# One piece of embedding weights serves all row blocks in the last weighted stage, half of its product is kept in SBUF, and an early split comes later

## The chip, the cores and the metric

The kernel runs on one core of one Trainium2 chip. Its time is the device time of one execution in microseconds (us); three executions of the kernel before gave a median of 803.88 us, from 803.66 to 804.14. One more execution was recorded by the profiler, and all rows of a profile come from that one.

The engines are named as the profile names them: PE is TensorE (matmuls; PEld is its weight loads), DVE is VectorE, ACT is ScalarE, POOL is GpSimd, SP is SyncE, which here only starts DMAs.

## The reference

With DEPTH = 1 the reference is one attention layer, a gated embedding, and a final normalization, over 512 rows of 2048 columns, all in float32:

```python
hn = rmsnorm(x, norm_g[0])
y = swa_mixer(hn, ...)            # windowed attention, out gated, @ w_out (2048 x 2048)
x = x + y
emb = p[0] @ ple_proj[0]          # 512 x 256 @ 256 x 2048
g = jax.nn.sigmoid(rmsnorm(x, ple_norm[0]) @ ple_gate[0])   # @ 2048 x 2048
x = x + emb * g
return rmsnorm(x, final_g)
```

The change touches the last four lines: the embedding `emb`, the gate `g`, and the final gain `final_g`.

## The kernel before

**Products in three parts.** Matmuls take operands that are rounded when written as `fp32r`. So each float32 operand is split in two: `hi` is a cast on ACT, `lo = raw - hi` a subtraction on DVE. `mm3` (lines 120 to 122) then makes one float32 product of three matmuls: hi·hi, hi·lo, lo·hi. A weight piece is 128 x 1024 (512 KB): it is loaded by SP (line 568), cast (line 575) and subtracted (line 576). The raw pieces, the `hi` and the `lo` parts have three buffers each (`wpool`, `bufs=3`). So the cast of piece n has to wait until PE is done with piece n-3.

**Seven products a stage.** The two 2048 x 2048 products (`w_out`, then `ple_gate`) are made by a scheme of seven block products instead of eight. A product p works on sums of quarters of the activations (`Forms`: again a cast, line 680, and a subtraction, line 681) and on sums of weight blocks. The last stage goes through p in the order 2, 7, 1, 6, 5, 3, 4. Each p but the last is two units, `jj` = 0 and 1, of 512 columns each. One unit takes four weight pieces m = 0..3, with 12 matmuls a piece: 48 matmuls into two banks of PSUM. After each piece it lets a share of the list `later` run (`some_later`), and then calls `todo()`, which issues a step of the next forms or an early split.

**Which product ends what.** With rows in four blocks t of 128 and columns in four groups j of 512, p = 1 ends the gate of rows t = 0, 1 and columns j = jj; p = 5 that of t = 2, 3 and j = 2 + jj; p = 3 that of t = 0, 1 and j = 2 + jj; p = 4, the last, that of t = 2, 3 and j = jj. Where a gate is complete, the embedding of the same rows and columns is needed. `embed` makes one block of it: six matmuls (two chunks of 128 of the contraction, three parts each) into one bank of PSUM, with a `ple_proj` piece of 512 columns that goes through the same queue of weight pieces (`add_embeds`). So for p = 1, 5 and 3 there are five pieces to a unit, and the columns 2 + jj come through the queue twice, once for p = 5 and once for p = 3.

**What follows a unit.** `gate` and `gated` (lines 890 to 905): ACT takes the sigmoid (line 896), DVE multiplies it with the embedding (line 898) and adds that to x (line 899), ACT takes the sum of squares (line 902). These steps are put at the front of `later`, and so run between the pieces of the next unit. Two sums go through `s2` and `s7`, tiles of 128 x 2 x 2 x 512.

**The last product.** Its eight weight pieces lie in SBUF before their turn and are split early by `split_last(k)` (lines 583 and 584), at places given by the table `early`: key (p, jj, m), value k. Then four blocks of 128 rows by 512 columns follow, each of 24 matmuls (`last`) and an embedding of 6; the fourth is made in two halves. Beside them the rows that are complete are normalized: a sum over `ssq3` (line 1034 for t = 0, 1), a root on ACT, then four multiplications by the root and the gain for t = 0 (line 920), four for t = 1, and so on, and the stores by SP (line 915). The gain is `final_g`, copied to all partitions in the tile `fg` (128 x 2048, 1 MB); its load is issued in the middle of the `w_out` stage, after p = 6 (line 870).

**What sets the order.** From the second product of the last stage on, the order of all engines is the order in which the program is written (`tc.manual_schedule` with PE, SP, DVE, Activation and Pool). Each engine runs its instructions in that order, and a wait holds up all that stands behind it on the same engine.

**PSUM.** There are four tags with two banks each: `p` and `s`, `t` and `o`. For p = 5 and 3 the two gate banks of a unit are those of p = 1, in `s` and `p`; the embeddings of unit jj go to tag `"to"[jj]`.

Of the kernel before, what the change touches and what calls it, by code (L numbers as in the profile page):

```python
# [20 lines left out]
P = 128  # L21
# [32 lines left out]
def trunk_kernel(ctx: ExitStack, tc: tile.TileContext, a: dict):  # L54
    nc = tc.nc
# [25 lines left out]
    def bank(name, tag):  # L81
        return others.get(tag, psum).tile([P, 512], F32, tag=tag, name=name)


    WE = 1024
# [31 lines left out]
    def mm3(ps, sh, sl, mh, ml, first, last, more=False):  # L117


        nc.tensor.matmul(ps, sh, mh, start=first, stop=False, skip_group_check=more)  # L120
        nc.tensor.matmul(ps, sh, ml, start=False, stop=False, skip_group_check=more)  # L121
        nc.tensor.matmul(ps, sl, mh, start=False, stop=last, skip_group_check=more)  # L122
# [23 lines left out]
    def run(gen):  # L146
        for _ in gen:
            pass
# [36 lines left out]
    for k in range(KC):  # L185
# [9 lines left out]
        room = acts if k < KC // 2 else more  # L195
# [14 lines left out]
        f, e = k == 0, k == KC - 1  # L210
# [8 lines left out]
        for t in range(2):  # L219
            c = slice(t * P, (t + 1) * P)  # L220
            mm3(kt_ps[t], wh[:, c], wl[:, c], h, l, f, e)
        for t in range(NB):
            c = slice(t * P, (t + 1) * P)
# [8 lines left out]
        if 3 <= k < 3 + NB:  # L232
            t = k - 3
# [190 lines left out]
    def turn(i):  # L424


        d, g = divmod(i, UNITS)
        pr = T.pop(i)
        pt = bank(f"pt{i}", "t")[:, :256]
        for u in range(2):  # L430
            nc.tensor.transpose(pt[:, u * P : (u + 1) * P], pr[:, u, :], ident)
        r = apool.tile([P, 2, 256], F32R, tag="r", name=f"r{i}", bufs=2)
        nc.scalar.copy(r[:, 0], pt)
        nc.vector.tensor_sub(r[:, 1], pt, r[:, 0].bitcast(F32))  # L434
        own = None
        if g >= 2:
            own = apool.tile([P, 2, 256], F32R, tag="own", name=f"own{i}", bufs=2)
            rows = slice(0, P) if g % 2 else slice(0, HB)
            flat = lambda v: v[rows].rearrange("p l (u q) -> p (l u) q", q=HB)


            sign = -1 if g % 2 else 1
            nc.gpsimd.affine_select(  # L443
                out=flat(own), in_=flat(r).bitcast(F32), pattern=[[0, 8], [sign, HB]], compare_op=ALU.is_ge, fill=0.0,
                base=-HB - 1 if g % 2 else 0, channel_multiplier=-sign,
            )
            here, there = slice(HB, P), slice(0, HB)
            if g % 2 == 0:
                here, there = there, here
            nc.scalar.copy(own[there, 0], own[here, 1].bitcast(F32))  # L450
        PT[i] = (r, own)
# [76 lines left out]
    def block(nm, r, c, jj, m):  # L528
        return a[nm][2 * (c - 1) + jj, 4 * (r - 1) + m]

    SUMS = [("w_out", 7), ("w_out", 5), ("w_out", 6), ("ple_gate", 7), ("ple_gate", 5)]
    for nm, p in SUMS:
        for jj in range(2):
            for m in range(4):
                t = summed[nm, p, jj, m] = tc.dram_tile([P, WE], F32, name=f"{nm}_{p}_{jj}_{m}")
# [12 lines left out]
    class Pieces:  # L548
# [38 lines left out]
        done = 0  # L587
# [26 lines left out]
    def add_stage(nm, order):  # L614
        at = {}

        def add_embeds(p, jj):
            if nm == "ple_gate" and p in (1, 5, 3, 4):
                j = jj + 2 * (p in (5, 3))
                B.add("proj", a["ple_proj"].rearrange("(k p) d -> p k d", p=P)[:, :, j * 512 : (j + 1) * 512])  # L620

        for p in order:
            for jj in range(2):
                if nm == "ple_gate" and (p, jj) == (4, 0):
                    for v in range(2):
                        at["e", v] = len(B.specs)
                        add_embeds(p, v)
                at[p, jj] = len(B.specs)
                for m in range(4):
                    if (nm, p) in SUMS:  # L630
                        src = summed[nm, p, jj, m]
                    else:
                        src = block(nm, *{1: (1, 1), 2: (2, 1), 3: (2, 2), 6: (1, 1), 4: (2, 1)}[p], jj, m)
                    growing = (6, 4) if (nm, 6) in SUMS else (7, 6, 4)
                    kind = "seed" if p == growing[0] else "grow" if p in growing else "one"
                    B.add(kind, src, (nm, jj, m) if p in growing else None)
                if p != 4:
                    add_embeds(p, jj)
        return at
# [112 lines left out]
    fg = late.tile([P, D], F32, name="fg")  # L752
# [17 lines left out]
    later = []  # L770
# [6 lines left out]
    def unit(p, jj, at, forms, todo):  # L777

        ps = banks(p, jj, forms.nm)
        f = forms.made[p]  # L780
        first = p not in (6, 5, 3)
        for m in range(4):
            bh, bl = B.get(at[p, jj] + m)
            for kk in range(2):
                k = 2 * m + kk
                fh, fl = f[m]
                for tb in range(2):
                    mm3(ps[tb], fh[:, kk, blk(tb)], fl[:, kk, blk(tb)], bh[kk], bl[kk], first and k == 0, k == 7, not first)
            some_later(4 - m)
            todo()  # L790
        return ps


    def load_x(j):
        nc.sync.dma_start(x1[j], a["x"].rearrange("(t p) d -> p t d", p=P)[:, :, j * 512 : (j + 1) * 512])
# [48 lines left out]
    for n, p in enumerate(ORDER_OUT):  # L844
        nxt = out_forms.steps(ORDER_OUT[n + 1]) if n < 6 else iter(())
        for jj in range(2):
            later.extend(held.pop(waiting.get((p, jj)), ()))
            calls = iter(range(4))

            def todo():  # L850
                part = x_at.get((p, jj, next(calls)))
                if part is not None:
                    load_x(part)
                next(nxt, None)
                if p == 4:
                    for tag in "to":
                        if turns:
                            turn(*turns.pop(0), tag)
                    if jj:
                        next(ple_first, None)  # L860

            ps = unit(p, jj, at_out, out_forms, todo)
            posts = [partial_of(add_y, p, jj, tb, ps[tb]) for tb in range(2)]
            if p == 1:
                held[p, jj] = posts
            else:
                later.extend(posts)
        run(nxt)
        if p == 6:
            nc.sync.dma_start(fg, a["final_g"].partition_broadcast(P))  # L870
        if p == 3:
            turns = [(kp, 0) for kp in range(8)] + [(kp, 1) for kp in range(4, 8)]
    run(ple_first)
# [8 lines left out]
    nc.vector.tensor_sub(pTl, pT, pTh.bitcast(F32))  # L882
    done = {t: 0 for t in range(NB)}

    def embed(t, w, tag, c=slice(0, 512)):
        e_ps = bank(f"e{t}_{done[t]}", tag)
        for k in range(2):
            mm3(e_ps[:, c], pTh[:, k, blk(t)], pTl[:, k, blk(t)], w[0][k][:, c], w[1][k][:, c], k == 0, k == 1)
        return e_ps
# [32 lines left out]
    s2, s7 = partial("s2"), partial("s7")  # L922
    turns = [(kp, 1) for kp in range(4)]

    def gate(p, jj, ps, e):
# [17 lines left out]
                zs.append((tb, 2 + jj, ps[tb], late.tile([P, 512], F32, tag="junk", name=f"z{jj}_{tb}", bufs=3)))  # L943
        return [gated(*z, e[z[0]]) for z in zs]

    def gate_later(*v):
        zs = gate(*v)
        later[:0] = [partial_of(next, z, None) for _ in range(3) for z in zs]
# [2 lines left out]

    spare = late.tile([P, 2 * WE], F32R, name="spare")
    rooms4 = {}
    early = {(5, 0, 3): 0, (5, 1, 2): 1, (5, 1, 3): 2, (3, 0, 1): 3, (3, 0, 3): 4, (3, 1, 0): 5, (3, 1, 2): 6}

    def split_last(k):
        if k == 0:
# [7 lines left out]
    for n, p in enumerate(ORDER_PLE[:-1]):  # L965
        if n == 1:

            ctx.enter_context(
                tc.manual_schedule(
                    engines={getattr(mybir.EngineType, v) for v in ("PE", "SP", "DVE", "Activation", "Pool")}  # L970
                )
            )
        nxt = ple_forms.steps(ORDER_PLE[n + 1])
        for jj in range(2):
            calls = iter(range(4))

            def todo():
                k = early.get((p, jj, next(calls)))
                if turns:
                    turn(*turns.pop(0), "s")  # L980
                    if not turns:
                        nc.vector.tensor_reduce(ss2, ssq2, axis=AX.X, op=ALU.add)
                        run(rsqrt_mean(rstd2, ss2, D, "r2"))
                    return
                next(nxt, None)
                if p == 2:
                    next(nxt, None)
                if k is not None:
                    split_last(k)

            ps = unit(p, jj, at_ple, ple_forms, todo)
            e = {}
            if p in (1, 5, 3):
                w = B.get(at_ple[p, jj] + 4)
                for t in (0, 1) if p in (1, 3) else (2, 3):
                    e[t] = embed(t, w, "to"[jj])
            if (p, jj) != (3, 1):
                later.insert(0, partial_of(gate_later, p, jj, ps, e))
        run(nxt)
# [4 lines left out]
    w = [B.get(at_ple["e", jj]) for jj in range(2)]  # L1004
    f = ple_forms.made[4]
# [155 lines left out]
```

## Time and profile before

| what | value |
| --- | --- |
| median of three executions | 803.88 us (803.66 to 804.14) |
| the profiled execution: time, span | 804.26 us, 802.4 us |
| PE busy | 791.1 us |
| PE weight loads busy | 660.0 us |
| DVE busy | 592.1 us |
| ACT busy | 500.5 us |
| POOL busy | 110.1 us |

The span goes from the first to the last instruction; the 1.9 us between span and time lie around it. A PE that is busy all the time is one whose matmuls follow each other; a wait of PE inside a stage shows as a longer step from one start to the next. In the last stage the matmuls of 512 columns start 0.227 us apart. A busy share over the span says little on single stages, so the stage of the change has to be read by its own rows.

### The profile page before, as it was taken

How to read it: one execution, taken by the hardware profiler on the slowest of the kernel's cores; microseconds unless marked ns; L12 is line 12 of the kernel's file. 1: busy time of each engine (PE TensorE's matmuls, PEld its weight loads, DVE VectorE, ACT ScalarE, POOL GpSimd, SP SyncE). 2: the span in 40 equal slices, each digit the busy share in tenths (PEclk: the TensorE clock that was granted, in tenths of full speed). 3: DMA queues.
4: the chain of work that ended last, by engine and by line, in shares of the span. 5: the costliest groups of instructions: out<-in, count | busy, mean ns of one | idle time of the engine just before them, and what ended most of it. 6: DMA issues, size and time to landing. Idle time of an engine off the chain costs nothing. (4 is left out here: it accounts for less than half of the span.)

```text
span 802.4 us, 10946 instructions
## 1 busy us (share of the span) xinstructions
PE 791.1 (99%) x3763; PEld 660.0 (82%) x3763; DVE 592.1 (74%) x970; ACT 500.5 (62%) x1041; POOL 110.1 (14%) x218
## 2 busy tenths in 40 slices
PE   9999999999999999999999999999999999999995
PEld 7888888888888888888888888888888888888785
DVE  4536886887777776777778897766646756989896
ACT  5624667676667666676666654655668656656855
POOL 0002213122122212112122200030000020200000
PEclk9999999999999999999999999999999999999998
DMA  8863678778687977868685369898513996785532
GB/s 318 327 172 101 183 241 215 228 202 233 172 220 215 218 215 199 221 177 246 159 219 132 105 233 348 333 275 248 195 46 92 372 216 197 156 229 182 182 107 105
DMA packets 45239, 165.15 MB, mean 206 GB/s; under 512 B 5936, under 2 KB 8112, under 8 KB 41344
## 3 DMA queue, kind: packets, MB, share of 16 engines
q1 hardware_dynamic: 38352, 130.59, 47.9%
q0 software_dynamic: 6832, 33.88, 22.4%
q8 instruction: 29, 0.48, 0.2%
q14 instruction: 26, 0.21, 0.1%
HBM read 158.63 MB, written 46.19 MB: 255 GB/s over the span
## 5 line engine op out<-in xcount | busy, mean ns | idle before, releaser
L576 DVE TENSOR_TENSOR blo<-braw,bhi 128x1024 fp32r<-128x1024 f32 x80 | 97.5, 1222 | 39.7 <-ACT bhi L575 39.4
L575 ACT CAST bhi<-braw 128x1024 fp32r<-128x1024 f32 x80 | 84.0, 1051 | 65.8 <-PE g L122 18.9
L122 PE MATMUL gps<-xh,wlo 128*128 128x512 f32 x256 | 100.1, 391 | 0.0
L121 PE MATMUL gps<-xl,whi 128*128 128x512 f32 x256 | 100.1, 391 | 0.0
L120 PE MATMUL gps<-xh,whi 128*128 128x512 f32 x256 | 99.8, 390 | 0.0
L107 DVE TENSOR_TENSOR wlo<-wraw,whi 128x1024 fp32r<-128x1024 f32 x60 | 73.3, 1221 | 20.8 <-ACT whi L106 19.7
L122 PE MATMUL qps<-xh,wlo 128*128 128x512 f32 x224 | 87.8, 392 | 0.0
L120 PE MATMUL o<-bhi,fho 128*128 128x512 f32 x224 | 87.7, 391 | 0.0
L121 PE MATMUL qps<-xl,whi 128*128 128x512 f32 x224 | 87.7, 391 | 0.0
L121 PE MATMUL o<-blo,fho 128*128 128x512 f32 x224 | 87.3, 390 | 0.0
L122 PE MATMUL o<-bhi,flo 128*128 128x512 f32 x224 | 87.2, 389 | 0.0
L120 PE MATMUL qps<-xh,whi 128*128 128x512 f32 x224 | 87.2, 389 | 0.0
L106 ACT CAST whi<-wraw 128x1024 fp32r<-128x1024 f32 x60 | 62.9, 1048 | 26.9 <-PE gps L121 10.6
L418 ACT ACTIVATE t<-t,sm 128x129 f32<-128x129 f32 x128 | 50.6, 397 | 45.9 <-DVE sm L415 45.6
L121 PE MATMUL g<-blo,fhg 128*128 128x512 f32 x192 | 75.0, 391 | 0.7 <-DVE blo L576 0.7
L120 PE MATMUL g<-bhi,fhg 128*128 128x512 f32 x192 | 75.1, 391 | 0.0
L122 PE MATMUL g<-bhi,flg 128*128 128x512 f32 x192 | 74.8, 390 | 0.0
L443 POOL TENSOR_SCALAR_AFFINE_SELECT own<-r 64x512 fp32r<-64x512 f32 (+1 forms) x48 | 34.1, 711 | 291.7 <-DVE r L434 286.2
L122 PEld LDWEIGHTS gps<-xh,wlo 128*128 128x128 f32 x256 | 48.0, 188 | 10.3
L576 DVE TENSOR_TENSOR blo<-grown,bhi 128x1024 fp32r<-128x1024 f32 x32 | 39.1, 1223 | 23.6 <-ACT bhi L575 21.9
L120 PEld LDWEIGHTS gps<-xh,whi 128*128 128x128 f32 x256 | 48.1, 188 | 8.9
L121 PEld LDWEIGHTS gps<-xl,whi 128*128 128x128 f32 x256 | 48.1, 188 | 8.9
(200 smaller groups left out, 1698.0 us busy)
## 6 DMA issues: line engine op xcount, KB each, us to landing
wraw<-in_w_gate_in SPq DMA_DIRECT2D x32, 512.0 KB, 5.6
wraw<-in_w_q SPq DMA_DIRECT2D x28, 512.0 KB, 4.5
w_out<-in_w_out POOLq DMA_DIRECT2D x24, 512.0 KB, 7.4
braw<-in_w_out SPq DMA_DIRECT2D x24, 512.0 KB, 4.3
braw<-in_ple_gate SPq DMA_DIRECT2D x24, 512.0 KB, 4.3
w_out<-in_w_out SPq DMA_DIRECT2D x16, 512.0 KB, 6.7
ple_gate<-in_ple_gate SPq DMA_DIRECT2D x16, 512.0 KB, 5.5
ple_gate<-in_ple_gate POOLq DMA_DIRECT2D x16, 512.0 KB, 7.2
```

What stands on the lines that cost most here:

```text
L106: nc.scalar.copy(hi, raw)
L107: nc.vector.tensor_sub(lo, raw, hi.bitcast(F32))
L120: nc.tensor.matmul(ps, sh, mh, start=first, stop=False, skip_group_check=more)
L121: nc.tensor.matmul(ps, sh, ml, start=False, stop=False, skip_group_check=more)
L122: nc.tensor.matmul(ps, sl, mh, start=False, stop=last, skip_group_check=more)
L418: nc.scalar.activation(su, su, AF.Exp, bias=sm[:, u : u + 1], accum_out=sm[:, 2 + u : 3 + u])
L443: nc.gpsimd.affine_select(out=flat(own), in_=flat(r).bitcast(F32), pattern=[[0, 8], [sign, HB]], compare_op=ALU.is_ge, fill=0.0, base=-HB ...
L575: nc.scalar.copy(hi, raw)
L576: nc.vector.tensor_sub(lo, raw, hi.bitcast(F32))
```

## The change

The `ple_proj` pieces of p = 3 are taken out of the queue of weight pieces. While the piece of columns 2 + jj is there for p = 5, the embeddings of all four row blocks are made with it. Those of t = 2, 3 are used from PSUM as before. Those of t = 0, 1 (named `k`) go to the other tag of embedding banks, `"to"[1 - jj]`, and `keep` copies them to SBUF by ACT: for jj = 0 into the first half of `fg`, for jj = 1 into `s7[:, 0]`. The gates of p = 3 multiply with these copies. The copies are a step of `later` that is put behind the steps of the unit's own gates.

Since `fg` is a room for the copies now, the load of `final_g` is moved from the `w_out` stage to the third piece of unit (3, 1).

Four of the early splits of the last weights come later: k = 3 from (3, 0, 1) to (3, 0, 3), k = 4 from (3, 0, 3) to (3, 1, 0), k = 5 from (3, 1, 0) to (3, 1, 1), k = 6 from (3, 1, 2) to (3, 1, 3).

```diff
@@ add_embeds
-            if nm == "ple_gate" and p in (1, 5, 3, 4):
-                j = jj + 2 * (p in (5, 3))
+            if nm == "ple_gate" and p in (1, 5, 4):
+                j = jj + 2 * (p == 5)
                 B.add("proj", a["ple_proj"].rearrange("(k p) d -> p k d", p=P)[:, :, j * 512 : (j + 1) * 512])
@@ the w_out stage
         run(nxt)
-        if p == 6:
-            nc.sync.dma_start(fg, a["final_g"].partition_broadcast(P))
@@ embed
-    def embed(t, w, tag, c=slice(0, 512)):
-        e_ps = bank(f"e{t}_{done[t]}", tag)
+    def embed(t, w, tag, c=slice(0, 512), nm="e"):
+        e_ps = bank(f"{nm}{t}_{done[t]}", tag)
@@ new
+    kept = {}
+
+    def keep(jj, e):
+
+        room = s7[:, 0] if jj else fg[:, :WE].rearrange("p (t c) -> p t c", t=2)
+        kept[jj] = [room[:, t] for t in range(2)]
+        for t in range(2):
+            nc.scalar.copy(kept[jj][t], e[t])
@@ the table of early splits
-    early = {(5, 0, 3): 0, (5, 1, 2): 1, (5, 1, 3): 2, (3, 0, 1): 3, (3, 0, 3): 4, (3, 1, 0): 5, (3, 1, 2): 6}
+    early = {(5, 0, 3): 0, (5, 1, 2): 1, (5, 1, 3): 2, (3, 0, 3): 3, (3, 1, 0): 4, (3, 1, 1): 5, (3, 1, 3): 6}
@@ todo
-                k = early.get((p, jj, next(calls)))
+                at = p, jj, next(calls)
+                k = early.get(at)
+                if at == (3, 1, 2):
+                    nc.sync.dma_start(fg, a["final_g"].partition_broadcast(P))
@@ after each unit
             e = {}
-            if p in (1, 5, 3):
+            if p in (1, 5):
                 w = B.get(at_ple[p, jj] + 4)
-                for t in (0, 1) if p in (1, 3) else (2, 3):
+                for t in (0, 1) if p == 1 else (2, 3):
                     e[t] = embed(t, w, "to"[jj])
+            if p == 3:
+                e = kept[jj]
+            if p == 5:
+
+                later.insert(0, partial_of(keep, jj, [embed(t, w, "to"[1 - jj], nm="k") for t in range(2)]))
             if (p, jj) != (3, 1):
                 later.insert(0, partial_of(gate_later, p, jj, ps, e))
```

## The prediction

> **What bounds the kernel now.** I read the page first, then the starts of PE's matmuls in the last stage, and then DVE's and ACT's own rows there, because a busy share is a mean over stages.
>
> The page's busy times (us, share of the span, instructions), and under them busy times by stretch: from a certain subtraction in unit (3, 0) to the reduction that opens the normalization of rows t = 0, 1, from there to the end of DVE's unbroken run, and on to the last gate.
>
> ```profile
> PE 791.1 (99%) x3763; PEld 660.0 (82%) x3763; DVE 592.1 (74%) x970; ACT 500.5 (62%) x1041; POOL 110.1 (14%) x218
> ```
> ```profile
> 738.78:771.02 32.24, 31.56 (x139) 25.57 (x138) 28.74 (x35) 23.72 (x37) 0.00 (x0) 1.00 0.41 135
> 771.02:784.56 13.54, 13.54 (x61) 11.20 (x61) 12.93 (x28) 6.07 (x10) 0.00 (x0) 1.00 0.48 156
> 784.88:792.71 7.83, 7.83 (x62) 7.61 (x61) 6.98 (x19) 4.84 (x9) 0.00 (x0) 1.00 0.41 134
> ```
>
> PE is full over the span. But in the last 60 us the third busy column, DVE, is as full: 28.74 of 32.24 us, then 12.93 of 13.54, then 6.98 of 7.83. Here two engines run side by side, and whichever is later sets the end. DVE's rows (start, duration, what it did, idle time before and its releaser):
>
> ```profile
> 737.64 2.35 DVE L576 TENSOR_TENSOR blo<-braw,bhi 128x1024 fp32r<-128x1024 f32 x2
> ...
> 762.50 0.68 DVE L898 TENSOR_TENSOR z<-e,z 128x512 f32<-128x512 f32 x1
> ...
> 771.02 0.15 DVE L1034 TENSOR_REDUCE ssum<-ssq 128x2 f32<-128x8 f32 x1
> ...
> 773.26 2.74 DVE L920 SCALAR_TENSOR_TENSOR x1s<-x1s,yn,fg 128x512 f32<-128x512 f32 x4
> ...
> 784.88 0.69 DVE L1018 TENSOR_TENSOR s<-last,s 128x512 f32<-128x512 f32 x1 [0.32 <-PE last L122]
> ...
> 792.23 0.42 DVE L1080 TENSOR_TENSOR x1s<-x1s,fg 128x256 f32<-128x256 f32 x1
> ```
> ```profile
> 792.55 0.13 PE last L122
> 792.71 0.43 DVE s L1018
> ```
>
> The first row holds two subtractions; the second starts at 737.64 + 2.35 - 1.22 = 738.77 (1.22 us is one subtraction of 1024, below), so one follows another after 1.13 us. From the reduction at 771.02 on, DVE works without a pause for PE until 784.88, where it waits 0.32 us: that is all its slack. In the chain of waits (second fence: start, length, work) the end hangs on PE's last block and the subtraction behind it at 792.71, while DVE's own row before it, from 792.23, ends at 792.65. So a DVE that is later by more than about 0.3 us at 771 is later at the end.
>
> PE's rows at the start of the embedding of unit (5, 0), at the first matmuls of unit (3, 1), and at the first of the last product:
>
> ```profile
> 720.95 0.39 PE L120 MATMUL e<-bhi,pTh 128*128 128x512 f32 x1
> ...
> 750.87 0.39 PE L120 MATMUL g<-bhi,fhg 128*128 128x512 f32 x1
> 751.93 0.50 PE L121 MATMUL g<-blo,fhg 128*128 128x512 f32 x1 [0.68 <-DVE blo L576]
> ...
> 765.64 0.39 PE L120 MATMUL last<-spare,fhg 128*128 128x512 f32 x1
> ```
>
> The second row is 132 matmuls behind the first, so they are 29.92 / 132 = 0.227 us apart; the next step is 1.06 us, where PE waits for the `lo` part of a weight piece: 0.83 us lost. Between the first and the last row lie 192 matmuls, 43.5 us at this pace, and they took 44.69: 1.16 us is PE's whole loss here.
>
> **The change part by part.**
>
> *PE.* The number of matmuls stays. The 24 of p = 3's embeddings go forward to p = 5, 12 behind each unit's own. A unit of p = 5 grows by 12 x 0.227 = 2.72 us, a unit of p = 3 shrinks by as much.
>
> *Removed:* two `ple_proj` loads of 512 KB on SP, their two casts on ACT and two subtractions on DVE. *Added:* four copies on ACT, PSUM to SBUF, of 128 x 512. The prices (duration min/median/max in ns for the copy; else busy us, mean ns):
>
> ```profile
> L931 ACT COPY s<-g x4: 579/590/604, 627.7 to 641.0; 128x512 f32<-128x512 f32 x4
> ```
> ```profile
> L576 DVE TENSOR_TENSOR blo<-braw,bhi 128x1024 fp32r<-128x1024 f32 x80 | 97.5, 1222 | 39.7 <-ACT bhi L575 39.4
> ```
>
> ACT gains two casts of 1.06 (row below) and pays 4 x 0.59: even. DVE gains two subtractions, 2 x 1.13 = 2.26 us of its queue. The four multiplications that now read the copy instead of PSUM I leave at their 0.68 us.
>
> *Where DVE starts.* This is the step that decides. The cast of the third piece of (3, 0) may overwrite a buffer only when PE is done with the `ple_proj` piece of (5, 1):
>
> ```profile
> 737.51 1.06 ACT L575 CAST bhi<-braw 128x1024 fp32r<-128x1024 f32 x1 [0.54 <-PE e L122]
> ```
>
> That piece is now held for all of p = 5's 24 extra matmuls: 24 x 0.227 = 5.44 us later. On top, the embedding of (5, 1) needs the two banks that hold the copies' sources of (5, 0). Those copies stand in ACT's queue behind a square that waits for DVE's addition. Setting each instruction behind its predecessor and its releasers, with the durations above, I get the first copy's end at 737.60, while PE wants the bank at 720.95 + 72 x 0.227 = 737.27: PE waits 0.36 us (bounds: 0, or both copies late, 0.9). So the cast starts at 737.51 + 5.44 + 0.36 = 743.31, the subtraction behind it 1.09 us later, at 744.40 instead of 738.77: 5.63 us late. The subtraction ahead of it is done at 741.4 by the same setting out, and the program's order holds all else behind this one: DVE idles 3 us.
>
> *What DVE still has to do before the reduction.* Before: 32.24 us from 738.78, 28.74 busy and 3.50 idle. After: the same list less two subtractions, 28.74 - 2.26 = 26.48. The early splits are moved but all stay within this stretch, so they cost nothing more; their deadline holds too, since the last one ends at about 773.7 and PE reads it only in the last quarter of the second block, about 775.7. Idle time is the unknown; bounds are 0 and the 3.50 of before. I set both queues out with the rows above and these of ACT (busy us, mean ns):
>
> ```profile
> L680 ACT CAST fhg<-hT 128x512 fp32r<-128x512 f32 x12 | 7.3, 611 | 1.2 <-DVE hT L668 1.2
> L583 ACT CAST last<-grown 128x1024 fp32r<-128x1024 f32 x7 | 7.3, 1043 | 0.0
> ...
> L896 ACT ACTIVATE s<-s,rstd 128x512 f32<-128x512 f32 x6 | 4.0, 714 | 0.0
> L902 ACT ACTIVATE s<-x1s 128x512 f32<-128x512 f32 x6 | 3.8, 631 | 3.1 <-DVE x1s L899 3.1
> ```
>
> Four waits for ACT come out: 0.74 at the last subtraction of the forms (ACT has two copies of the second `keep` ahead of that form's cast), 0.35 and 0.50 at the early splits k = 3 and 5 (two sigmoids ahead), 0.78 at k = 6 (two squares ahead), with some 0.2 of small ones 2.58. I take that: it lies between the bounds, nearer to before. The reduction then stands at 744.40 + 26.48 + 2.58 = 773.46, 2.44 us late.
>
> *The tail.* DVE no longer waits for PE at 784.88: -0.32. In its place the root of row block 2 is late by itself, since ACT loads a table for it (start, duration):
>
> ```profile
> 783.88 1.28 ACT L158 ACT_TABLE_LOAD   x1
> 785.17 0.20 ACT L158 ACTIVATE rt_r<-ms_r 128x1 f32<-128x1 f32 x1
> ```
>
> From the last addition ahead of it ACT needs a square, this load and the root, 0.2 us more than DVE needs for what stands in between; the wait for PE had covered that: +0.23. The rest is the same list. So DVE is late by 2.35 us at the last subtraction. PE gets to the last product at 720.95 + 43.5 + 0.36 = 764.8, 0.8 us earlier than before, and then has to wait for nobody, but it doesn't set the end any more.
>
> *The load of `final_g`.* Its old place costs nothing to leave: PE waits for nothing there. At its new place SP holds it until the second multiplication with the first copy is done, which stood at 762.50, 8.52 us ahead of the reduction; with one subtraction less and the 0.78 us wait in between it is 8.17 ahead: 773.46 - 8.17 + 0.68 = 766.0. Behind it on SP stand only the stores, the first after the rows below. The rows of t = 0 need it 2.24 us after the reduction (773.26 before), at 775.7: a window of 9.7 us. Loads of 1 MB (KB, median us to landing), and DMA share and GB/s (last two columns) where the old load ran and where the new one will:
>
> ```profile
> x1s<-in_x SPq DMA_DIRECT2D x4, 1024.0 KB, 7.0
> ...
> fg<-in_final_g SPq DMA_DIRECT2D x1, 1024.0 KB, 17.2
> ```
> ```profile
> 765.70:776.00 10.30, 10.30 (x47) 8.55 (x46) 9.72 (x20) 6.94 (x11) 0.00 (x0) 1.00 0.12 43
> 518.00:536.00 18.00, 18.00 (x81) 14.92 (x80) 12.27 (x14) 9.90 (x14) 5.15 (x6) 1.00 1.05 324
> ```
>
> The bounds are 7.0 and 17.2 us. The 17.2 were taken with the DMA engines at 1.05, the new place has 0.12; I take 7.0, which is hidden. [...]
>
> *Sum.* +2.35 us on the profiled execution, 804.26 to 806.6; that execution lies 0.4 us above the median, so from the median 803.88 + 2.35 = 806.2 us.
>
> **The rivals.**
>
> *PE sets the end (not slower).* If the idle time that I gave DVE vanishes, 2.58 us, DVE is late by -0.2 and PE's 0.8 us gain is what is left to see: 803.1 us. For it speaks that PE's one real wait goes, and two subtractions with it; against it the table of stretches, where DVE has no slack, and the 3 us hole that opens ahead of it. It decides below a lateness of 0.3 us. The Trainium skill, Perfetto Trace Analysis, section Identifying the Most-Contended Engine, takes the engine of highest occupancy as the one to improve, for TensorE by its weight loads; with 82% against DVE's 74% that rule points to this rival, while the stretches above speak for DVE.
>
> *`final_g` lands late.* From 9.7 us on, each us of landing is one us at the end, since rows t = 0 stand in DVE's queue ahead of all else. At 12 us: 808.5; at 17.2: 813.7. For it speaks the only row of this very load; against it the quiet DMA engines.
>
> *DVE is late by less.* The same mechanism with half of the idle time: late by 2.35 - 1.29 = 1.06 us, 804.9.
>
> **How the numbers follow.** 0.2% is 1.6 us, about what a measurement of this kernel can tell from no change. DVE late by more than 1.6 us: 0.60; by less: 0.16; PE sets the end: 0.11, of which 0.04 for more than 1.6 us of gain; `final_g` late: 0.13. Slower 0.73, same 0.23, faster 0.04. The likeliest case by itself reaches from 805.5 to 807.2 (idle as before, 0.92 more, 3.27 in all). The range goes from 804.2 to 808.2: it leaves out the case of PE and a late landing beyond 11.7 us.
>
> **What would show it.** Right: in the changed kernel DVE idles about 3 us ahead of the third subtraction of (3, 0), behind a cast released by PE at about 743; PE's wait at 751 is gone and one of some 0.4 us stands before the second embedding of p = 5; the reduction of `ssum` is at 773 to 774; DVE doesn't wait for PE at the last blocks, and PE's last matmul ends 2 us or more before the last subtraction that reads it. Wrong: the reduction near 771, or a wait of `x1s` rows for the DMA of `fg`, or PE waiting again in p = 3.

## The result and the profile after

The changed kernel takes 806.49 us in the median (805.41 to 808.19, eleven executions); the kernel before, in executions beside it, 804.10 (803.53 to 805.52, eleven). The ratio is 1.0028, with a 95% interval of 1.0019 to 1.0038: slower by 1.5 to 3.1 us, and by 2.4 us in the middle.

The profiled execution of the changed kernel has a time of 805.41 us and a span of 803.5 us. It is the shortest of its eleven, so its span can't be set against the other span directly. The part ahead of the last stage differs from one profile to the next by up to 2 us. Its code is the same in both kernels but for the load of `final_g`, and that load doesn't show there: in the seven profiles of this document with the load ahead of the stage, the mark named below stands at 721.04 us on average, in the seven without it at 721.11. I therefore measure from one mark, the first embedding matmul of unit (5, 0), to the end of the span, and call that the distance. Before: 802.4 - 720.95 = 81.45 us. After, by the first row of the next fence: 803.5 - 720.44 = 83.06 us, which is 1.61 us more.

PE's rows of the changed kernel (start, duration, operation): the mark, the last matmul ahead of the embeddings of (5, 1) with the first two of them, and the last matmul of all. Under them the last matmul of the kernel before.

```profile
720.44 0.39 PE L120 MATMUL e<-bhi,pTh 128*128 128x512 f32 x1
...
736.53 0.39 PE L122 MATMUL g<-bhi,flg 128*128 128x512 f32 x1
737.00 0.50 PE L120 MATMUL e<-bhi,pTh 128*128 128x512 f32 x1
737.33 0.40 PE L121 MATMUL e<-blo,pTh 128*128 128x512 f32 x1
...
791.80 0.28 PE L122 MATMUL e<-bhi,pTl 128*128 128x256 f32 x1
```
```profile
793.11 0.28 PE L122 MATMUL e<-bhi,pTl 128*128 128x256 f32 x1
```

PE is faster: its last matmul stands 71.36 us behind the mark, and 72.16 before. The 0.8 us forecast for PE are there, and the wait at 751 is gone. The step at 737.00 is 0.47 us and the next 0.33, instead of 0.227 each: PE waits 0.34 us for the bank of a copy's source (ACT's first copy of unit (5, 0) ends at 736.96).

DVE's rows of the changed kernel (start, duration, operation, and in brackets the idle time before with its releaser), and its busy times by stretch (the columns are those of the prediction's second fence):

```profile
739.56 1.22 DVE L576 TENSOR_TENSOR blo<-braw,bhi 128x1024 fp32r<-128x1024 f32 x1
743.90 1.23 DVE L576 TENSOR_TENSOR blo<-braw,bhi 128x1024 fp32r<-128x1024 f32 x1 [3.12 <-ACT bhi L575]
...
754.72 0.69 DVE L681 TENSOR_TENSOR flg<-hT,fhg 128x512 fp32r<-128x512 f32 x1 [0.53 <-ACT fhg L680]
755.67 1.22 DVE L584 TENSOR_TENSOR low<-grown,last 128x1024 fp32r<-128x1024 f32 x1 [0.26 <-ACT last L583]
...
760.61 1.23 DVE L584 TENSOR_TENSOR low<-grown,last 128x1024 fp32r<-128x1024 f32 x1 [0.32 <-ACT last L583]
...
767.36 1.23 DVE L584 TENSOR_TENSOR low<-grown,last 128x1024 fp32r<-128x1024 f32 x1 [0.60 <-ACT last L583]
...
772.30 0.16 DVE L1049 TENSOR_REDUCE ssum<-ssq 128x2 f32<-128x8 f32 x1
...
786.70 0.16 DVE L160 RECIPROCAL y_r<-rt_r 128x1 f32<-128x1 f32 x1 [0.25 <-ACT rt_r L158]
...
793.78 0.42 DVE L1033 TENSOR_TENSOR s<-last,s 128x256 f32<-128x256 f32 x1
```
```profile
743.90:772.30 28.40, 28.40 (x127) 23.50 (x126) 26.49 (x32) 22.91 (x37) 0.00 (x0) 1.00 0.36 130
772.30:785.51 13.21, 13.21 (x63) 11.06 (x62) 12.63 (x26) 5.74 (x10) 0.00 (x0) 1.00 0.49 159
785.51:793.78 8.27, 6.57 (x55) 6.37 (x54) 7.19 (x22) 5.51 (x9) 0.00 (x0) 1.00 0.38 128
```

The hole is where the prediction put it: DVE is done with the subtraction of 739.56, then idles 3.12 us behind a cast. That cast, on ACT, and PE's last matmul on the `ple_proj` piece of (5, 1):

```profile
742.34 0.39 PE L122 MATMUL k<-bhi,pTl 128*128 128x512 f32 x1
```
```profile
742.81 1.05 ACT L575 CAST bhi<-braw 128x1024 fp32r<-128x1024 f32 x1 [3.48 <-issue]
```

The trace names no releaser for the cast (`issue`). But it starts 0.08 us after that matmul ends (742.34 + 0.39 = 742.73), as the cast at 737.51 did in the kernel before, where the trace names PE. From the hole on DVE's list is nearly without gaps, 26.49 of 28.40 us. In the third row PE is busy for only 6.57 of 8.27 us, because it has run out of work while DVE goes on. The chain of waits of the changed kernel (start, length, work) says the same: the last subtraction hangs on DVE's own instruction before it, not on PE's last block as it did.

```profile
793.45 0.41 DVE x1s L1095
793.87 0.34 DVE s L1033
```

### The profile page after: what moved, and what is told of

It is laid out like the page before. It is cut to its first block, busy times and chain, and to the rows that moved or that the text cites. A ratio compares the mean times of both kernels' runs of the same rounds, so it can differ in the third digit from the quotient of the medians.

```text
span 803.5 us, 10939 instructions
## 1 busy us (share of the span) xinstructions
PE 791.2 (98%) x3763; PEld 661.0 (82%) x3763; DVE 589.7 (73%) x968; ACT 500.2 (62%) x1043; POOL 110.6 (14%) x218
## 4 chain that ended last, share of the span: by engine, by line
PE 94%; DVE 3%; ACT 1%; issue 1%; DVEq 0%
PE gps L122 7%; PE gps L121 7%; PE gps L120 7%; PE qps L122 7%; PE qps L121 7%; PE qps L120 7%; PE o L121 6%; PE o L120 6%; PE o L122 6%; PE g L120 5%; PE g L122 5%; PE g L121 5%; PE s L389 3%; PE o L467 2%; PE vps L227 2%; PE pt L431 2%
## 5 line engine op out<-in xcount | busy, mean ns | idle before, releaser
L576 DVE TENSOR_TENSOR blo<-braw,bhi 128x1024 fp32r<-128x1024 f32 x78 | 95.3, 1222 | 43.1 <-ACT bhi L575 43.1
L575 ACT CAST bhi<-braw 128x1024 fp32r<-128x1024 f32 x78 | 82.1, 1052 | 68.3 <-PE o L122 18.0
```

Of the source, the lines that this page charges most:

```text
L575: nc.scalar.copy(hi, raw)
L576: nc.vector.tensor_sub(lo, raw, hi.bitcast(F32))
```

## The experiments

Most of them change one thing in the changed kernel. All distances are worked out as above, from the mark and the span of each run's profile, one profile a run; the second column is the distance from the mark to the start of the reduction that opens the normalization.

| kernel | mark to reduction, us | mark to end, us | ratio to the kernel before, 95% interval |
| --- | --- | --- | --- |
| before | 50.07 | 81.45 | |
| changed | 51.86 | 83.06 | 1.0028, 1.0019 to 1.0038 |
| e1 own room, `final_g` early | 51.86 | 83.14 | 1.0029, 1.0017 to 1.0040 |
| e2 early splits into the hole | 50.85 | 82.11 | 0.9999, 0.9991 to 1.0008 |
| e3 changed, old table | 51.19 | 82.42 | 1.0004, 0.9995 to 1.0014 |
| e4 before, new table | 49.47 | 80.65 | 1.0002, 0.9989 to 1.0014 |
| e5 more DVE work ahead of the hole | 51.86 | 83.10 | 1.0025, 1.0014 to 1.0035 |
| e6 more DVE work behind the hole | 53.12 | 83.94 | 1.0024, 1.0013 to 1.0034 |
| e7 rows to POOL, changed | 55.07 | 85.05 | 1.0039, 1.0026 to 1.0051 |
| e8 rows to POOL, before | 51.58 | 82.22 | 1.0012, 1.0004 to 1.0021 |
| e9 rows left out, changed | 51.91 | 80.75 | 0.9986, 0.9976 to 0.9996 |
| e10 rows left out, before | 49.79 | 81.24 | 0.9997, 0.9989 to 1.0006 |
| e11 half of the change | 50.85 | 82.00 | 1.0005, 0.9996 to 1.0014 |
| e12 before, new table, again | 49.33 | 80.53 | 0.9992, 0.9984 to 1.0001 |

**Does the late load of `final_g` matter?** The copies of jj = 0 get a tile of their own, and the load goes back to its old place. An unused tile, `pad`, shrinks from 32 to 16 columns in this run; that line and other context are left out below.

```diff
@@ the w_out stage
+        if p == 6:
+            nc.sync.dma_start(fg, a["final_g"].partition_broadcast(P))
@@ keep
+    own = late.tile([P, WE], F32, name="own")
-        room = s7[:, 0] if jj else fg[:, :WE].rearrange("p (t c) -> p t c", t=2)
+        room = s7[:, 0] if jj else own.rearrange("p (t c) -> p t c", t=2)
@@ todo
-                if at == (3, 1, 2):
-                    nc.sync.dma_start(fg, a["final_g"].partition_broadcast(P))
```

> The changed kernel with a room of its own for the first pair of copies, and the load of final_g back at its old place after p = 6 of the w_out stage. In the profile of the changed kernel that load landed 4.3 us after its issue and nobody waited for it. Theory (DVE late: the end is set by DVE's queue, which loses 3.1 us ahead of the third subtraction of (3, 0)): the load costs nothing, so 2.4 us over the kernel before as the changed kernel, within 0.6, and in the trace the reduction of ssum at the same distance, 28 to 29 us, behind that third subtraction. Rival (the load at its new place is late in executions that the profile did not catch): at most 0.5 us over the kernel before.

Nothing changes: 51.86 us to the reduction and 83.14 to the end, and the ratio is the same. That rival is out. The load itself, in the rows of the tile `fg` in the changed kernel (an issue of 341 ns at 764.9, and the time to landing), took 4.3 us:

```profile
L988 SPq DMA_DIRECT2D fg<-in_final_g x1: 341/341/341, 764.9 to 764.9; - x1
...
DMA to landing us min/median/max: 4.3/4.3/4.3
```

**Can the hole be filled?** The splits k = 3 and 4 move to the place of k = 2, ahead of the subtraction that waits; the function runs all the splits of an entry.

```diff
-    early = {(5, 0, 3): 0, (5, 1, 2): 1, (5, 1, 3): 2, (3, 0, 3): 3, (3, 1, 0): 4, (3, 1, 1): 5, (3, 1, 3): 6}
+    early = {(5, 0, 3): (0,), (5, 1, 2): (1,), (5, 1, 3): (2, 3, 4), (3, 1, 1): (5,), (3, 1, 3): (6,)}
```

> The changed kernel with the early splits k = 3 and 4 moved ahead into (5, 1, 3), so that ACT and DVE have them to do while they wait for PE to let go of the ple_proj piece; k = 5 and 6 stay. Theory (DVE late): the two subtractions, 2 x 1.13 us, go into the hole of 3.1 us, which shrinks to about 0.8; part of it comes back as waits for ACT in (3, 0) and (3, 1), since there is less DVE work to cover the sigmoids and squares. Set out by hand: the end 1.2 us earlier than in the changed kernel, so 1.2 us over the kernel before, with 0.1 as the bound if nothing comes back. Rival (final_g late) and rival (PE's order costs it): no change, 2.4 us over the kernel before.

DVE's rows of this run, from the splits in the hole to the reduction:

```profile
738.66 3.86 DVE L584 TENSOR_TENSOR low<-grown,last 128x1024 fp32r<-128x1024 f32 x3 [0.43 <-ACT last L583]
742.44 1.22 DVE L576 TENSOR_TENSOR blo<-braw,bhi 128x1024 fp32r<-128x1024 f32 x1
744.15 1.22 DVE L576 TENSOR_TENSOR blo<-braw,bhi 128x1024 fp32r<-128x1024 f32 x1 [0.49 <-ACT bhi L575]
...
771.54 0.16 DVE L1049 TENSOR_REDUCE ssum<-ssq 128x2 f32<-128x8 f32 x1
```

The wait goes from 3.12 to 0.49 us, with two more splits ahead of it (the first row holds k = 2, 3 and 4). The reduction comes 1.01 us sooner and the end 0.95 us. The time can't be told from that of the kernel before; the distance is still 0.66 us over it. Of the 2.3 us of work that went into the hole, 1 us arrives at the reduction: behind it the splits k = 5 and 6 and a subtraction still wait 0.60 to 0.87 us each for ACT.

**Which side of the hole counts?** The subtraction of one split is done twice: k = 2, ahead of the hole, or k = 7, behind it. I expected 1.13 us more in DVE's queue for each; the runs show 1.27 and 1.26.

```diff
@@ split_last, e5: (2,), e6: (7,)
             nc.vector.tensor_sub(lo, raw, hi.bitcast(F32))
             self.made[i] = tuple([t[:, :512], t[:, 512:]] for t in (hi, lo))
+            if k in (2,):
+                nc.vector.tensor_sub(lo, raw, hi.bitcast(F32))
```

> The changed kernel with the subtraction of the early split k = 2 made twice: 1.13 us more for DVE, placed just ahead of the hole in front of the third piece of (3, 0). Theory (DVE late, by the hole): the hole takes it up, 3.1 us become 2.0, and the end is where it is in the changed kernel: 83.1 us from the first embedding matmul of (5, 0) to the end of the span, within 0.3. Rival (DVE's whole work sets the end, the hole is covered by something else): 1.1 us later, 84.2.

> The changed kernel with the subtraction of the early split k = 7 made twice: the same 1.13 us more for DVE, now behind the hole, just ahead of the reduction of ssum. Theory (DVE late): the end is 1.0 to 1.1 us later than in the changed kernel, 84.1 us from the first embedding matmul of (5, 0) to the end of the span. Rival (PE sets the end): no change, 83.1.

Ahead of the hole the work is free. The hole shrinks from 3.12 to 1.85 us, and both distances stay (51.86 and 83.10):

```profile
744.05 1.23 DVE L576 TENSOR_TENSOR blo<-braw,bhi 128x1024 fp32r<-128x1024 f32 x1 [1.85 <-ACT bhi L575]
```

Behind the hole the reduction comes 1.26 us later, and the end 0.88 us. The difference is mostly a wait of DVE for the root of rows t = 0, 1, right behind the reduction: 0.31 us in the changed kernel, none in this run. The medians, 806.40 and 806.51, don't tell these two kernels apart; the distances do.

**The table of early splits alone.** Once the old table in the changed kernel (the lines below, shortened), and twice the new table in the kernel before (the same edit backwards).

```diff
-    early = {..., (3, 0, 3): 3, (3, 1, 0): 4, (3, 1, 1): 5, (3, 1, 3): 6}
+    early = {..., (3, 0, 1): 3, (3, 0, 3): 4, (3, 1, 0): 5, (3, 1, 2): 6}
```

> The changed kernel with the table of early splits of the kernel before: only the embedding and the load of final_g are changed. Theory (DVE late): the same DVE work, but k = 3 falls into (3, 0, 1) again, where the waits for ACT are smaller; set out by hand 0.8 us less than the changed kernel, 1.6 us over the kernel before, with a wait of PE of 0.2 us at the second piece of (3, 1). Rival (the later splits are needed, PE would stall without them): 2.4 us or more over the kernel before.

> The kernel before with the later early splits alone. Theory (DVE and PE both set the end, DVE by its whole list): the DVE list is as long as before, so the time stays within 0.4 us, although PE's wait of 0.83 us at the start of (3, 1) goes. Rival (PE alone sets the end): 0.8 us faster.

> The kernel before with the changed kernel's early table alone, a second time, since one look and its times did not agree (distance 0.8 us shorter, ratio 1.0002). If the later table is a gain by itself in the kernel before (PE's wait of 0.7 us at the first pieces of unit (3, 1) goes, and DVE waits less for ACT): distance 80.4 to 80.9 us and a ratio of 0.9985 to 0.9995. If the first look was an accident of the loads: distance 81.2 to 81.7, ratio 0.9995 to 1.0010.

In the kernel before, the later table shortens the distance by 0.80 us in one run and by 0.92 in the other, and PE's wait at 751 is gone in both. That is the rival's number; my bound of 0.4 us was too low. The times follow only in part, with ratios of 1.0002 and 0.9992, whose intervals hold 1. So the table alone is probably a gain of some tenths of a microsecond, and not shown to be one in time.

In the changed kernel the same move costs: with the old table the distance is 0.64 us shorter. The step that I priced at nothing, "the early splits are moved but all stay within this stretch, so they cost nothing more", costs that much. The reason isn't the one that I expected, a smaller wait at k = 3. From the hole to the reduction DVE's waits of 0.53, 0.26 and 0.32 us are the same with the old table; the fourth, 0.60 us ahead of k = 6, is missing. With the old table k = 6 comes one piece earlier, ahead of the two squares, and DVE doesn't wait for its cast:

```profile
766.81 1.22 DVE L584 TENSOR_TENSOR low<-grown,last 128x1024 fp32r<-128x1024 f32 x1
```

So the table is a part of the slowdown. With the old table the changed kernel is still 0.97 us over the kernel before by distance, but its time can't be told from it (1.0004, up to 1.0014): what the held piece costs without the table's 0.64 us is shown by the distances, not by the times.

**Half of the change.** Only the piece of (5, 1) makes all embeddings; (3, 0) loads its own piece as before; `final_g` loads at its old place.

```diff
@@ against the changed kernel: add_embeds
-            if nm == "ple_gate" and p in (1, 5, 4):
-                j = jj + 2 * (p == 5)
+            if nm == "ple_gate" and (p in (1, 5, 4) or (p, jj) == (3, 0)):
+                j = jj + 2 * (p in (5, 3))
@@ after each unit
-            if p in (1, 5):
+            if p in (1, 5) or (p, jj) == (3, 0):
...
-            if p == 3:
+            if (p, jj) == (3, 1):
                 e = kept[jj]
-            if p == 5:
+            if (p, jj) == (5, 1):
```

> Half of the change: only the piece of unit (5, 1) makes the embeddings of all rows, and only its half is kept (in the room of the second sum); unit (3, 0) loads its piece and makes its embeddings as before, final_g is loaded at its old place, the early table is that of the changed kernel. The piece of (5, 1) is then held by 12 matmuls more instead of 24. Theory (the hole ahead of the third subtraction of (3, 0) is the time for which PE holds that piece longer, less DVE's work ahead of it): the subtraction starts 2.72 us later than before against the first embedding matmul instead of 5.63, DVE idles 0.6 to 1.2 us ahead of it instead of 3.12, does one subtraction less (1.13), and the distance from the first embedding matmul to the end is 81.0 to 81.7 us (before 81.45, changed 83.06); time within 1 us of the kernel before. Rival (the hole comes from the order of the queues and not from the time that the piece is held): 2 us or more of idle time ahead of the subtraction and a distance of 82.5 or more.

The mark and PE's last matmul on the piece, the cast that takes its buffer, and DVE's third subtraction of (3, 0) and the reduction in this run:

```profile
720.50 0.39 PE L120 MATMUL e<-bhi,pTh 128*128 128x512 f32 x1
...
739.32 0.39 PE L122 MATMUL k<-bhi,pTl 128*128 128x512 f32 x1
```
```profile
739.79 1.05 ACT L575 CAST bhi<-braw 128x1024 fp32r<-128x1024 f32 x1 [3.26 <-issue]
```
```profile
740.87 1.23 DVE L576 TENSOR_TENSOR blo<-braw,bhi 128x1024 fp32r<-128x1024 f32 x1 [2.46 <-ACT bhi L575]
...
771.35 0.15 DVE L1049 TENSOR_REDUCE ssum<-ssq 128x2 f32<-128x8 f32 x1
```

The cast starts 0.08 us after that matmul ends, here too. It stands 19.29 us behind the mark; before it was 737.51 - 720.95 = 16.56, and in the changed kernel 742.81 - 720.44 = 22.37. So 12 more matmuls on the piece make it 2.73 us late, which is 12 x 0.227, and 24 make it 5.81, which is 24 x 0.227 and PE's wait of 0.34 for the bank. The delay is the time for which PE holds the piece longer. The subtraction behind it stands at 20.37, 17.82 before (738.77 - 720.95) and 23.46 in the changed kernel (743.90 - 720.44), so 2.55 and 5.64 late: about 0.17 less each, because before it followed its cast not at once but 0.17 us later, behind DVE's own subtraction.

The hole is larger than I expected (2.46 us, not 0.6 to 1.2), as large as the rival wanted it, and the end lies 0.3 us above my bounds and 0.5 below the rival's. I had taken the time at which DVE reaches the hole from the changed kernel, where DVE is held up once more, 2.53 us, ahead of a subtraction of unit (5, 1); in this run that wait is 0.37 us, so DVE gets to the hole sooner and waits there. What speaks against the rival is the start of the cast, not the size of the hole.

**Is DVE really the end?** The four multiplications of rows t = 1 are taken off DVE. The first attempt gave the gain to POOL, ahead of the reduction, and the root to ACT.

```diff
+    for j in range(4):
+        nc.gpsimd.tensor_mul(x1[j][:, 1, :], x1[j][:, 1, :], gain(j))
     yn2 = const.tile([P, 3], F32, name="yn2")
...
-    for j in range(4):
-        row(1, j, yn2[:, 1:2])
-        store(1, j)
     g = block(1, 0, "s", "t")()
     next(g)
+    for j in range(4):
+        nc.scalar.mul(x1[j][:, 1, :], x1[j][:, 1, :], yn2[:, 1:2])
+        store(1, j)
```

> The changed kernel with the four multiplications of rows t = 1 by root and gain taken off DVE: the gain by POOL, the root by ACT behind the sigmoid of the second block; 4 x 0.67 = 2.7 us less for DVE in the tail. Theory (DVE late): 2.0 us earlier by hand, until PE and the chain from the last matmul on set the end again: 81.1 us from the first embedding matmul of (5, 0) to the end of the span, and about 0.4 us over the kernel before. Rival (PE sets the end): no change, 83.1. POOL's price isn't shown in any run yet; its four multiplications have 5 us before ACT wants them, so about 1.3 us each would still be hidden.

> The kernel before with the same four multiplications taken off DVE. Theory (in the kernel before PE and DVE end together, with 0.3 us between them): 0.4 us earlier at most, 81.1 us from the first embedding matmul of (5, 0) to the end of the span (81.45 in the kernel before). Rival (the kernel before is as much bound by DVE as the changed one): 2 us earlier, 79.5.

Both came out longer than without this edit, the changed kernel by 1.99 us and the kernel before by 0.77. POOL's row and DVE's beside it, in the changed kernel with this edit:

```profile
770.77 6.98 POOL L1048 TENSOR_TENSOR x1s<-x1s,fg 128x512 f32<-128x512 f32 x4 [63.23 <-DMA fg<-in_final_g]
```
```profile
770.28 0.69 DVE L897 TENSOR_TENSOR x1s<-x1s,z 128x512 f32<-128x512 f32 x1
770.88 1.78 DVE L896 TENSOR_TENSOR z<-s,z 128x512 f32<-128x512 f32 x1
772.70 1.66 DVE L897 TENSOR_TENSOR x1s<-x1s,z 128x512 f32<-128x512 f32 x1
774.29 2.31 DVE L584 TENSOR_TENSOR low<-grown,last 128x1024 fp32r<-128x1024 f32 x1
776.52 0.15 DVE L1051 TENSOR_REDUCE ssum<-ssq 128x2 f32<-128x8 f32 x1
776.71 1.07 DVE L157 TENSOR_SCALAR ms_r<-ssum 128x2 f32<-128x2 f32 x1
```

While POOL works, four of DVE's instructions take about 1 us longer each (1.78 and 1.66 instead of 0.68, 2.31 instead of 1.22, 1.07 instead of 0.17): 4.1 us lost, against 2.7 saved. POOL had to wait for `final_g`, which lands late in this kernel, so all four of its multiplications fell there. In the kernel before, about half of the 0.77 us is a longer wait of PE at 751 (1.05 us for 0.68), and the rest lies behind the last subtraction. So these two runs say nothing on what they were for. The second attempt leaves the multiplications out, with nothing in their place; the rows of t = 1 are then stored without their norm and gain.

```diff
     for j in range(4):
-        row(1, j, yn2[:, 1:2])
         store(1, j)
```

> The changed kernel with the four multiplications of the second row block in the last embedding stage (2.73 us on DVE in its trace) left out: that block is stored without its gain and norm, so the output is not the reference's. Unlike the run that moved them to POOL, nothing takes their place. Theory (DVE sets the end of the changed kernel): the last subtraction starts 1.7 to 2.4 us earlier against the first embedding matmul, held then by PE, and the distance from that matmul to the end of the span falls from 83.06 to between 80.7 and 81.4 us; the time falls by about 2 us, to within 0.5 of the kernel before or below it. Rival (PE, or the transfers, set the end): the distance stays above 82.5 and the time within 0.6 us of the changed kernel's 806.5.

> The same four multiplications left out of the kernel before, which likewise leaves one row block without its gain and norm. Theory (there the last part of the work waits for PE in places, so that DVE's time is only partly on the path): DVE gains at most the 0.4 us that its last subtraction stands after PE, distance 81.0 to 81.5 us against 81.45, time within 0.5 us of the kernel before. Rival (DVE alone sets the end of both kernels): 2 us or more less here as well, distance 79.5 or under, time near 802.

These two runs decide. Without 2.73 us of DVE's work the changed kernel's distance falls by 2.31 us, to 80.75, and the kernel before's by 0.21, to 81.24; of the 0.21, 0.17 is a shorter wait of PE at 751 in that run (0.51 us for 0.68). The changed kernel, slower by 2.4 us, is now faster than the kernel before as it stands (ratio 0.9986, 0.9976 to 0.9996). The mark of this run, and the chain of waits at its last subtraction (start, length, work):

```profile
721.75 0.39 PE L120 MATMUL e<-bhi,pTh 128*128 128x512 f32 x1
```
```profile
792.48 0.12 PE last L121
792.60 0.14 PE last L122
792.74 0.02 issue
792.76 0.44 DVE s L1033
```

PE releases the last subtraction again, 71.01 us behind the mark; before it was 792.71 - 720.95 = 71.76. The 0.75 us between them are PE's gain, which the late DVE had covered. In the kernel before, leaving them out only lets DVE wait for PE, 2.12 us at one block:

```profile
784.22 0.69 DVE L1018 TENSOR_TENSOR s<-last,s 128x512 f32<-128x512 f32 x1 [2.12 <-PE last L122]
```

## Why the prediction was right, and where it was off

The mechanism was the one forecast: PE gains, DVE ends later, DVE sets the end. The forecast was 806.2 us, the median is 806.49. By the distances the profiled execution grew by 1.61 us and the last subtraction by 73.34 - 71.76 = 1.58 (793.78 - 720.44 after), not by the 2.35 of the sum. The interval of the ratio, 1.5 to 3.1 us, holds both numbers, so the good median is partly luck. Of the signs given, the hole, PE's waits and DVE without a wait for PE at the last blocks came; the reduction, set at 773 to 774, came at 772.30, which is 772.81 counted from the mark of the kernel before.

*Where DVE starts (5.63 us late).* 5.64 by the mark. PE's wait for the bank is 0.34 us, taken as 0.36. Half of the change shows what the delay is made of. This part is no luck.

*What DVE has to do (26.48 us).* 26.49. The copies took 576 ns for 590, and the two multiplications in this stretch that read the copies in `fg` 685 ns, as those that read PSUM.

*Idle time to the reduction (2.58 us).* This is the term that was mis-sized: 28.40 - 26.49 = 1.91 us. The four waits are where I set them, each shorter: 0.53 for 0.74, 0.26 for 0.35, 0.32 for 0.50, 0.60 for 0.78. Ahead of the cast that each of them waits for, ACT has instructions that I set one behind the other at their full durations. ACT's rows of the changed kernel show that they follow faster (the first three lines belong to the first two waits, then two lines to the third, three to the fourth; ahead of k = 3 stands the form's cast, not the two sigmoids that the prediction has there):

```profile
753.11 1.05 ACT L951 COPY s<-k 128x512 f32<-128x512 f32 x2
754.05 0.63 ACT L680 CAST fhg<-hT 128x512 fp32r<-128x512 f32 x1
754.58 1.06 ACT L583 CAST last<-grown 128x1024 fp32r<-128x1024 f32 x1
...
758.37 1.27 ACT L894 ACTIVATE z<-g,rstd 128x512 f32<-128x512 f32 x2
759.52 1.06 ACT L583 CAST last<-grown 128x1024 fp32r<-128x1024 f32 x1
...
765.67 0.63 ACT L900 ACTIVATE z<-x1s 128x512 f32<-128x512 f32 x1 [0.61 <-DVE x1s L897]
766.21 0.18 ACT L900 ACTIVATION_READ_ACCUMULATOR z<-x1s 128x1 f32 x1
766.30 1.03 ACT L583 CAST last<-grown 128x1024 fp32r<-128x1024 f32 x1
```

From the first start to the next instruction two copies take 0.94 us, by full durations 2 x 0.59 = 1.18; the form's cast 0.53 for 0.61; two sigmoids 1.15 for 2 x 0.71 = 1.42; a square with its second instruction 0.63 for 0.81. That is 0.24, 0.08, 0.27 and 0.18 us less, and the waits are 0.21, 0.09, 0.18 and 0.18 shorter. For DVE I had used the step (1.13 for 1.22), for ACT the duration. That this is the whole cause of the missing 0.67 us is argued from the rows; no run isolates it.

*The moved splits, at nothing.* Their run showed 0.64 us, nearly all of it the wait of 0.60 ahead of k = 6. The sum over DVE's list contains that wait already as idle time (0.78 at k = 6), so it is an error of the reason given and not of the sum.

*The tail (-0.09 us).* From the reduction to the last subtraction 793.78 - 772.30 = 21.48 us, before 21.69: -0.21. The wait for PE is gone, and the root of row block 2 waits 0.25 us, forecast as 0.23. What the forecast left out is the last subtraction itself: before, PE held it, and it started 0.48 us behind the instruction ahead of it (792.23 to 792.71); now it starts 0.33 us behind (793.45 to 793.78).

*PE (0.8 us earlier).* 0.80, and hidden; where the rows of t = 1 are left out, 0.75 of it shows at the last subtraction.

*The load of `final_g` (7.0 us, hidden).* 4.3 us, hidden; in the other six runs with the load at its new place 4.2 to 6.6 us, in the seven with it at the old place (DMA share 1.05 in the prediction's rows) 13.6 to 19.4. The Trainium skill, DMA: Bandwidth & Descriptors, section Anatomy of one DMA — SWDGE (gpsimd) path, fits 2.0 us plus bytes over 436 GB/s, by estimate 4.4 us for 1 MB. That fit is for DMAs that GpSimd issues; this load is issued by SP, so no run here tests it.

*The rivals.* "PE sets the end" fell. The rule of the Trainium skill, Perfetto Trace Analysis, section Identifying the Most-Contended Engine, pointed to it with 82% against 74%. Those are the shares of the kernel before, and there the runs without the rows of t = 1 agree with the rule: 2.73 us less of DVE's work were worth 0.21 us. In the changed kernel the shares are almost the same, 82% and 73%, and they disagree: there the 2.73 us were worth 2.31 us at the end. "`final_g` lands late" fell with the run that gives the copies their own room. "DVE is late by less", the same mechanism with half of the idle time, is nearer to the profile (1.06 us forecast, 1.61 measured) than the forecast is (2.35); by the times it is the other way round.

No version is shown to beat both kernels: the new table in the kernel before has the shortest distance of all that do the whole work (80.65 and 80.53 us), and a time that can't be told from the kernel before's.

## What to carry to other kernels

Ask of every piece of work that is moved forward on an engine which buffer it now holds longer, and who is queued behind that buffer's next writer: here 24 matmuls, no more than before in number, cost DVE a hole of 3 us through one buffer of a ring of three. Judge what an engine's hole costs by the stretch behind it: work ahead of the hole was free, the same work behind it cost 0.9 to 1.3 us. Where an instruction is moved, look at what now stands ahead of it on the engine that it waits for: one split placed behind two squares cost 0.6 us. When a queue is set out by hand, use the step from one start to the next, not the duration, for every engine.

## What was not expected of the hardware

A multiplication on POOL held up DVE. Beside POOL's four (6.98 us, 1.75 each on average) DVE's instructions of two SBUF inputs took 0.97 to 1.10 us longer each, and a TENSOR_SCALAR of 128x2 0.9. In the kernel before with the same edit, one POOL instruction was enough to hold up one of DVE's, and DVE's ended as POOL's did, at 773.4:

```profile
771.94 1.45 POOL L1033 TENSOR_TENSOR x1s<-x1s,fg 128x512 f32<-128x512 f32 x1 [5.71 <-ACT z L902]
```
```profile
772.35 1.07 DVE L157 TENSOR_SCALAR ms_r<-ssum 128x2 f32<-128x2 f32 x1
```

The Trainium skill, SBUF — State Buffer, section Terms, says of the port pair that DVE and GpSimd share that it is held for a whole instruction and that the loser "fully blocks"; these rows agree. Moving work from DVE to POOL was no relief here: 2.7 us saved, 4.1 us lost.

The other surprise is the size of what can't be seen: executions of one kernel differ by 2 us and more, as much as the effect. The distance from a mark inside the stage was steadier and told apart what the medians did not. To the reduction it was 51.86 to 51.91 us in four profiles of the changed kernel that should be alike up to there. In the kernel before it is less steady, 50.07 and 49.79 us in two that should be alike, so there a few tenths of a microsecond show nothing.
